# An encoder layer on one core: the output projections with eight pairs of k tiles by seven products instead of five, and weight sums formed by accumulating transfers

## The chip, the cores and the metric

The kernel runs on one core of a Trainium2 chip. The metric is the device time of one execution in microseconds (us); three runs of the kernel before gave a median of 909.48 us (908.48 to 910.48).

TensorE (PE) does the matmuls, VectorE (DVE) and ScalarE (ACT) the elementwise work, GpSimd (POOL) a few small operations, and SyncE (SP) issues the DMA transfers. Each engine works through its own queue in order; semaphores hold an instruction until what it reads, or the buffer that it writes, is ready.

## The reference

One encoder layer on 512 rows of width 1024 in float32: a feed-forward block (FFN), a mixer (a convolution and an mLSTM), and a second FFN. The change touches only the two FFNs, and in them only the second matrix product, `@ w_out`:

```python
def swiglu(x, w_in, w_out):
    gate, up = jnp.split(x @ w_in, 2, axis=-1)      # x: 512 x 1024, w_in: 1024 x 5632
    return (jax.nn.silu(gate) * up) @ w_out         # 512 x 2816 by 2816 x 1024

h = swiglu(rmsnorm(x, norm_ffn1_pre[l]), w_ffn1_in[l], w_ffn1_out[l])
x = x + FFN_RESIDUAL_SCALE * rmsnorm(h, norm_ffn1_post[l])
...
h = swiglu(rmsnorm(x, norm_ffn2_pre[l]), w_ffn2_in[l], w_ffn2_out[l])
x = x + FFN_RESIDUAL_SCALE * rmsnorm(h, norm_ffn2_post[l])
```

## The kernel before, in words

**Three matmuls for a float32 product.** Every operand is split into a high part (a cast on ScalarE, L295) and the rest (a subtraction, mostly on VectorE, L297); the product is high by high, high by low and low by high, all into one accumulator. So every weight tile and every left side passes ScalarE and VectorE once before PE may use it.

**Fewer products.** A product of two by two blocks takes seven block products instead of eight in the manner of Strassen, if sums of blocks are formed first. The first projection does that throughout (`mm_part`, L434; sums of its weights L159). The second projection, the subject here, has 22 k tiles of 128 rows. A pair of k tiles (2n, 2n+1) with the two halves of the rows and the two halves of the 1024 columns makes such a two by two product: 7 x 2 x 3 = 42 matmuls of 512 columns (`product_out`, L567), where the two plain k tiles (`mm_out`, L592) take 24 each. `SEVEN` = 5 pairs are done so, k tiles 10 to 21 plainly.

**The order.** All accumulators of the second projection fit in the eight banks of PSUM only if the products share them, so the pairs are gone through twice. In phase "a" PE does products 1, 5, 6 and 7 of all five pairs (24 matmuls each), then `taken` copies those four sums out (ScalarE copies L577 and L579, VectorE sums L534), and in phase "b" it does products 2, 3 and 4 (18 matmuls each), each pair followed by one plain k tile (10 to 14). Then come k tiles 15 and 16, and last the five k tiles 17 to 21 (`TAIL`), one block of 128 rows after the other, each followed by its norm. The list `OUT` holds this order:

```python
    OUT = [("a", i) for i in range(SEVEN)]
    for i in range(SEVEN):
        OUT += [("b", i), ("k", 2 * SEVEN + i)]
    OUT += [("k", k) for k in range(3 * SEVEN, NF)]
```

**The weights' way.** `w_load` issues the loads in the order of the list `stream` (SP, L146 and L148) into four buffers `raw` (512 KB each); `w_get` makes the high and low parts of weights loaded earlier and starts the next loads, one or two entries ahead. For a pair, call the blocks of its weight B11, B12 (first k tile, left and right columns), B21 and B22 (second). In "a" a pair loads its first k tile and the right half of the second; `w_out_a` forms B12-B11, B22-B12 and B22-(B12-B11) with three VectorE subtractions (L192), and keeps the last in a small buffer. In "b" the second k tile is loaded whole, and `w_out_b` forms B21 minus the kept one (L215).

**The left sides.** `left_a` and `left_b` form sums of column halves of the activations, 128x256 at a time (L534), and split them, for one pair at a time.

**What sets the order within an engine.** The program is written once, and a scheduler with a cost model puts each engine's instructions in an order before the kernel is built; on the chip the queues run in that order. A buffer of a pool is handed on when its last reader is done, and a load into it waits for that.

**Where it stands.** In the profiled execution PE begins the first FFN's output projection at 231.46 us; the preparation of its first weights on ScalarE and VectorE overlaps the end of the first projection.

Of the kernel before, what the change touches and what calls it, by code (L numbers as in the profile page):

```python
# [28 lines left out]
TAIL = 5  # L29
SEVEN = 5  # L30
# [8 lines left out]
def encoder_kernel(ctx: ExitStack, tc: tile.TileContext, a: dict, out: bass.AP):  # L39
# [93 lines left out]
    stream = [v if isinstance(v[0], list) else one(v) for v in stream]  # L133
    loaded, ready = [], []
    pos, done = [0], [0]

# [48 lines left out]
    kept = []  # L185

    def w_out_a(r0, r1):
# [3 lines left out]
        def sub(o, a_, b_):  # L191
            nc.vector.tensor_tensor(out=o, in0=a_, in1=b_, op=ALU.subtract)  # L192
# [12 lines left out]
        split(bh[:, c[0]], bl[:, c[0]], r1[:, c[0]])  # L205
        split(bh[:, c[1]], bl[:, c[1]], t)
        return {1: (ah[:, c[0]], al[:, c[0]]), 7: (ah[:, c[1]], al[:, c[1]]),
                5: (bh[:, c[0]], bl[:, c[0]]), 6: (bh[:, c[1]], bl[:, c[1]])}

    def w_out_b(r1):  # L210
# [4 lines left out]
        nc.vector.tensor_tensor(out=r1[:, c[0]], in0=r1[:, c[0]], in1=kept.pop(0), op=ALU.subtract)  # L215
        split(t[:, c[0]], t[:, c[1]], r1[:, c[0]])
# [221 lines left out]
    def ffn(xq, between, finish, mid=None, within=None, ahead=(2, 2, 1, 1), late=None, prep=None):  # L438
# [3 lines left out]
        h = [bigt() for _ in range((NF + 3) // 4)]  # L442

# [80 lines left out]
        ea, eb = bigt(), bigt()  # L524
# [15 lines left out]
        def parts(hi, lo, at):  # L540
            return {n: (hi[:, c:c + 256], lo[:, c:c + 256]) for n, c in at.items()}

        def left_a(i):
            a_, b_ = hcol(2 * i), hcol(2 * i + 1)
            hi, lo = halves()
            s1 = t4()[:, 0:256]
            tt(s1, a_[:, early], b_[:, early], ALU.add)
            split(hi[:, 0:256], lo[:, 0:256], a_[:, later])
            tt(a_[:, early], a_[:, later], a_[:, early], ALU.subtract)
            tt(a_[:, later], s1, a_[:, later], ALU.subtract)  # L550
            split(hi[:, 256:512], lo[:, 256:512], s1)
            split(hi[:, 512:1024], lo[:, 512:1024], a_)
            return parts(hi, lo, {1: 0, 5: 256, 7: 512, 6: 768})

        def left_b(i):
            a_, b_ = hcol(2 * i), hcol(2 * i + 1)
            hi, lo = halves()
            split(hi[:, 0:512], lo[:, 0:512], b_)
            tt(a_[:, early], b_[:, later], a_[:, later], ALU.subtract)
            split(hi[:, 512:768], lo[:, 512:768], a_[:, early])  # L560
            return parts(hi, lo, {4: 0, 2: 256, 3: 512})
# [614 lines left out]
```

## Time and profile before

| | |
|---|---|
| median of 3 runs | 909.48 us (908.48 to 910.48) |
| the profiled execution | 911.16 us |
| its span in the trace | 909.4 us |
| granted TensorE clock, whole span | 0.999 |
| bytes moved by DMA | 96.47 MB, mean 106 GB/s |
| share of the 16 DMA engines' time, loads and stores | 35.5% |

The profile gives, for each engine, the time in which it was busy; the program's work on PE is so dense that its pieces overlap, so a mean duration of one matmul (0.39 us) is longer than the distance from one to the next. Windows give the busy time of each engine in a stretch of the span, with the number of its instructions in brackets; the chain of waits is followed back from the last instruction to whatever released each step; a row of an instruction names start, duration, engine, line, operation, and output <- input, and in square brackets the idle time just before it with what ended it. `ps` are PSUM accumulators, `whi` and `wlo` high and low parts of weights, `raw` loaded weights, `big` large buffers (four times 512 columns), `t` small ones.

### The profile page before, as it was taken

The page shows a single profiled execution, that of the slowest core. Times are in us where ns is not written, and L with a number is a line of the kernel's source. Part 1 is how long each engine was busy: PE and PEld are TensorE (multiplying, and loading weights), DVE is VectorE, ACT ScalarE, POOL GpSimd, SP SyncE. Part 2 cuts the span into 40 slices and gives each one's busy share as a digit, 9 for nine tenths or more (in the row PEclk, how much of TensorE's full clock was granted, in tenths as well). Part 3 has the DMA queues.
Part 4 walks back from the last instruction along what each step waited for, and adds up shares of the span by engine and source line. Part 5 has one row for each costly group of instructions (what it writes and reads, how often), then busy time and mean ns, then how long its engine had stood idle before and what let it go on. Part 6 is the DMA issues. An engine that isn't in the chain of part 4 may idle for free.

```text
span 909.4 us, 14920 instructions
## 1 busy us (share of the span) xinstructions
PE 896.4 (99%) x5971; PEld 814.5 (90%) x5971; DVE 691.1 (76%) x1115; ACT 460.2 (51%) x807; POOL 42.5 (5%) x68
## 2 busy tenths in 40 slices
PE   9999999999999999999999999999999999999997
PEld 7999999999877888988888888999999999977885
DVE  5988988888999457474666647889888988999435
ACT  6645555555565434464555435545545545566311
POOL 5000000000001001100011000000000000000000
PEclk9999999999999999999999999999999999999999
DMA  8233434333344650433222602224443432343402
GB/s 240 85 95 116 138 96 133 100 94 105 116 140 121 188 157 1 120 91 95 71 67 73 205 0 80 61 70 117 116 117 93 121 107 88 118 146 108 161 2 92
DMA packets 126256, 96.47 MB, mean 106 GB/s; under 512 B 4181, under 2 KB 114793, under 8 KB 126186
## 3 DMA queue, kind: packets, MB, share of 16 engines
q1 hardware_dynamic: 126186, 95.51, 35.5%
q8 instruction: 47, 0.77, 0.3%
q14 instruction: 23, 0.19, 0.1%
HBM read 93.40 MB, written 2.10 MB: 105 GB/s over the span
## 4 chain that ended last, share of the span: by engine, by line
PE 91%; DVE 4%; DMA 2%; ACT 1%; issue 1%; DVEq 0%; POOLq 0%; POOL 0%; ACTq 0%
PE ps L434 39%; PE ps L592 13%; PE ps L425 12%; PE ps L567 9%; PE ps L456 5%; PE ps L1133 5%; PE ps L755 3%; DMA raw<-in_w_ffn_in_dram 2%; DVE big L297 1%; DVE wlo L297 1%; PE ps L346 1%; PE ps L1048 1%; DVE big L534 1%; ACT big L295 1%; PE ps L288 1%
## 5 line engine op out<-in xcount | busy, mean ns | idle before, releaser
L297 DVE TENSOR_TENSOR wlo<-raw,whi 128x1024 fp32r<-128x1024 f32 x203 | 240.0, 1192 | 49.3 <-ACT whi L295 25.7
L295 ACT CAST whi<-raw 128x1024 fp32r<-128x1024 f32 x207 | 207.4, 1029 | 123.6 <-DVE raw L159 48.1
L434 PE MATMUL ps<-big,whi 128*128 128x256 f32 x1920 | 264.8, 280 | 0.3 <-ACT whi L295 0.2
L434 PEld LDWEIGHTS ps<-big,whi 128*128 128x128 f32 x1920 | 243.0, 188 | 1.2 <-ACT whi L295 0.7
L434 PE MATMUL ps<-big,wlo 128*128 128x256 f32 x960 | 151.2, 280 | 0.0
L434 PEld LDWEIGHTS ps<-big,wlo 128*128 128x128 f32 x960 | 129.5, 188 | 0.0
L592 PE MATMUL ps<-whi,big 128*128 128x512 f32 x384 | 121.8, 394 | 0.4 <-ACT whi L295 0.4
L592 PEld LDWEIGHTS ps<-whi,big 128*128 128x128 f32 x384 | 71.9, 188 | 17.3 <-ACT whi L295 1.3
L425 PE MATMUL ps<-big,whi 128*128 128x512 f32 x320 | 78.3, 397 | 0.0
L567 PE MATMUL ps<-whi,big 128*128 128x512 f32 x240 | 75.2, 392 | 2.7 <-ACT big L295 2.7
L592 PE MATMUL ps<-wlo,big 128*128 128x512 f32 x192 | 75.0, 393 | 0.0
L425 PEld LDWEIGHTS ps<-big,whi 128*128 128x128 f32 x320 | 59.5, 188 | 13.7 <-issue 0.2
L434 PE MATMUL ps<-big,ws 128*128 128x256 f32 x480 | 65.3, 280 | 0.0
L434 PEld LDWEIGHTS ps<-big,ws 128*128 128x128 f32 x480 | 60.2, 188 | 0.0
L567 PEld LDWEIGHTS ps<-whi,big 128*128 128x128 f32 x240 | 44.7, 188 | 12.9 <-ACT big L295 3.5
L504 ACT COPY t<-ps 128x256 f32<-128x256 f32 x40 | 14.9, 372 | 70.9 <-PE ps L434 70.7
L295 ACT CAST big<-big 128x512 fp32r<-128x512 f32 (+2 forms) x68 | 36.1, 582 | 23.5 <-DVE big L534 10.8
L567 PE MATMUL ps<-wlo,big 128*128 128x512 f32 x120 | 44.6, 391 | 0.0
L592 PEld LDWEIGHTS ps<-wlo,big 128*128 128x128 f32 x192 | 36.1, 188 | 8.3
L297 DVE TENSOR_TENSOR big<-big,big 128x512 fp32r<-128x512 f32 (+2 forms) x68 | 40.6, 634 | 0.0
L425 PE MATMUL ps<-big,wlo 128*128 128x512 f32 x160 | 40.4, 395 | 0.0
L425 PEld LDWEIGHTS ps<-big,wlo 128*128 128x128 f32 x160 | 30.0, 188 | 7.0
(207 smaller groups left out, 1130.4 us busy)
## 6 DMA issues: line engine op xcount, KB each, us to landing
raw<-in_w_ffn_in_dram SPq DMA_DIRECT2D x88, 512.0 KB, 5.0
raw<-in_w_ffn_out_dram SPq DMA_DIRECT2D x44, 512.0 KB, 4.5
raw<-in_w_mix_in_dram SPq DMA_DIRECT2D x24, 512.0 KB, 6.0
raw<-in_w_mix_out_dram SPq DMA_DIRECT2D x8, 512.0 KB, 3.7
raw<-in_w_ffn_out_dram SPq DMA_DIRECT2D x10, 256.0 KB, 3.4
out_dram<-x SPq DMA_DIRECT2D x8, 256.0 KB, 2.0
x<-in_x_dram SPq DMA_DIRECT2D x4, 256.0 KB, 5.1
x<-in_x_dram SPq DMA_DIRECT2D x2, 512.0 KB
```

Source lines behind the costliest of these rows:

```text
L288: pin(nc.tensor.matmul(pw[:, 0:256], warm[:, 0:P], warm, start=True, stop=True))
L295: latest["hi"] = nc.scalar.copy(out=hi, in_=src)
L297: latest["lo"] = eng.tensor_tensor(out=lo, in0=src, in1=f32(hi), op=ALU.subtract)
L346: pin(nc.tensor.transpose(out=pt[:, blk(k)], in_=xs[:, blk(4 * b + k)], identity=ident))
L425: nc.tensor.matmul(o, ww[:, k, :], xk(xT, xx, k, sl), start=n == 0, stop=n == 3 * KD - 1)
L434: pin(nc.tensor.matmul(o, ww[:, k, :], x[xx][:, k, :], start=first and n == 0, stop=n == 11, skip_group_check=True))
L456: pin(nc.tensor.matmul(o, ww[:, k, :], xq_hl(xq, (k // 4, th))[xx][:, k % 4, :], start=n == 0, stop=n == 3 * KD - 1))
L504: nc.scalar.copy(a_[:, h1], x[:, h0])
L567: nc.tensor.matmul(acc[tb + t][half], left[n][x][:, blk(t)], right[n][y], start=first and x == y == 0, stop=last_ and x == 1, skip_group_c ...
L592: nc.tensor.matmul(acc[tb][half], hT[hh][:, blk(tb)], w[ww][:, blk(half, 512)], start=fresh and hh == ww == 0, stop=k == NF - 1 and hh == ...
L755: nc.tensor.matmul(pv_[i][:, 0:at.stop - at.start], xk(xT, xx, k, blk(tb)), ww[:, k % 2, at], start=n == 0, stop=n == 3 * KD - 1)
L1133: nc.tensor.matmul(acc[half], yy[yi][:, k % 4, blk(tb)], wmo[k][wi][:, blk(half, 512)], start=(n == 0 and yi == 0 and wi == 0), stop=(n == ...
```

## The change

Eight pairs (k tiles 0 to 15) are done by seven products; k tile 16 is the only plain one between, after the first pair of "b", and 17 to 21 remain the tail. The signs in the seven products are chosen anew, so that the weights' combinations are plain sums: products 1, 5, 6 and 7 use B11, B11+B12, B11+B12+B22 and B12+B22, products 2, 3 and 4 use B21, B22 and B11+B12+B21+B22.

The sums come about in transfers. SP loads B11 and B22 side by side into one `raw`, and a transfer issued by POOL with `accum_op` add then adds B12 to both (L148): the buffer holds B11+B12 and B12+B22. SP loads B11 once more by itself (L159; the first two pairs into a small `t` tile, later ones into four slots of a large one, `ring`). One VectorE addition (L225) makes B11+B12+B22 of B11 and the right half, into a kept buffer; in "b" a second accumulating transfer adds B21 to it (L164), and the second k tile is loaded whole as before. The left sides are formed for two pairs at a time, 128x2x256 in place of 128x256 (L561), into two large buffers instead of one, and `taken` subtracts where it added. The load of the gate weights for the stage that follows (`mid`) is started at the first plain k tile, now 16 instead of 12. The pools keep their sizes.

```diff
-SEVEN = 5
+SEVEN = 8
...
-        OUT += [("b", i), ("k", 2 * SEVEN + i)]
-    OUT += [("k", k) for k in range(3 * SEVEN, NF)]
+        OUT += [("b", i)] + [("k", 2 * SEVEN + i)] * (2 * SEVEN + i < NF - TAIL)
+    OUT += [("k", k) for k in range(2 * SEVEN, NF) if ("k", k) not in OUT]
...
-                stream.append(([w_out[blk(2 * n), :], w_out[blk(2 * n + 1), 512:1024]], "a"))
+                stream.append(((w_out[blk(2 * n), :], w_out[blk(2 * n + 1), :]), "a"))
...
+                if kk == "a":
+                    top, low = aps
+                    sums = rawp.tile([P, 1024], F32, tag="raw", name=nm("raw"))
+                    nc.sync.dma_start(sums[:, 0:512], top[:, 0:512])
+                    nc.sync.dma_start(sums[:, 512:1024], low[:, 512:1024])
+                    nc.gpsimd.dma_start(
+                        sums.rearrange("p (g f) -> p g f", g=2), 
+                        top[:, 512:1024].rearrange("p (g f) -> p g f", g=1).broadcast_to([P, 2, 512]), accum_op=ALU.add)
...
+                    nc.sync.dma_start(own, top[:, 0:512])
+                    raws = [own, sums]
+                    loaded.append((raws, kk))
+                    continue
+                if kk == "b":
+                    nc.gpsimd.dma_start(kept[0], aps[0][:, 0:512], accum_op=ALU.add)
...
+                    own = [kept.pop(0)]
...
-        sub(r1[:, c[0]], r0[:, c[1]], r0[:, c[0]])
-        sub(r0[:, c[1]], r1[:, c[1]], r0[:, c[1]])
-        t = t2()
-        sub(t, r1[:, c[1]], r1[:, c[0]])
+        t = keep()
+        nc.vector.tensor_tensor(out=t, in0=r0, in1=r1[:, c[1]], op=ALU.add)
         kept.append(t)
         ah, al = wt("whi"), wt("wlo")
-        split(ah, al, r0)
+        split(ah[:, c[0]], al[:, c[0]], r0)
         bh, bl = wt("whi"), wt("wlo")
-        split(bh[:, c[0]], bl[:, c[0]], r1[:, c[0]])
-        split(bh[:, c[1]], bl[:, c[1]], t)
...
+        split(bh, bl, r1)
+        split(ah[:, c[1]], al[:, c[1]], t)
...
         split(hi, lo, r1)
-        nc.vector.tensor_tensor(out=r1[:, c[0]], in0=r1[:, c[0]], in1=kept.pop(0), op=ALU.subtract)
-        split(t[:, c[0]], t[:, c[1]], r1[:, c[0]])
+        split(t[:, c[0]], t[:, c[1]], t4_)
...
         def left_a(i):
-            a_, b_ = hcol(2 * i), hcol(2 * i + 1)
-            hi, lo = halves()
-            s1 = t4()[:, 0:256]
-            tt(s1, a_[:, early], b_[:, early], ALU.add)
-            split(hi[:, 0:256], lo[:, 0:256], a_[:, later])
...
+            g, a_, b_ = group(i)
+            hi, lo = halves(g)
+            s1 = t4()[:, 0:256 * g].rearrange("p (g f) -> p g f", g=g)
+            tt(s1, a_[:, :, early], b_[:, :, early], ALU.subtract)
+            split(hi[:, :, 0:256], lo[:, :, 0:256], a_[:, :, later])
...
-                if n == 12 and mid:
+                if plain_n == 1 and mid:
                     mid()
```

**VectorE at the end of the first projection of the first FFN.** The first pairs' weight sums stand among the splits of the last first-projection weights (`wlo_27..` and `ws_..`) and the rows that finish its results (L506 to L512, later L531 to L537). A name in the last brackets is a semaphore waited for: DMAHW one of SP's transfers, DMASW one of POOL's. Before:

```order
L192 TENSOR_TENSOR raw_2871<-raw_2869 128x512 [waits DMAHW3_49]
L297 TENSOR_TENSOR ws_372_2759<-t_369_2750,ws_372_2759 128x512 [waits Activation_49]
L511 TENSOR_TENSOR t_365_2651<-ps_2647,t_365_2651 128x256 [waits PE_49]
L159 TENSOR_TENSOR raw_2746<-t_369_2750,raw_2746 128x512 [waits DVE_49]
L192 TENSOR_TENSOR raw_2869<-raw_2871,raw_2869 128x512 [waits DMAHW4_49,DVE_49]
L512 TENSOR_TENSOR big_230<-t_365_2651,t_366_2652 128x256 [waits DVE_49]
L159 TENSOR_TENSOR raw_2746<-raw_2746 128x512 [waits DVE_49]
L508 TENSOR_TENSOR t_382_2775<-ps_2772,t_380_2773 128x256 [waits PE_49]
L297 TENSOR_TENSOR wlo_2763<-raw_2746,whi_2762 128x1024 [waits Activation_49]
L487 TENSOR_TENSOR big_230<-ps_2647,t_366_2652 128x256 [waits PE_49]
```

and now:

```order
L186 TENSOR_TENSOR raw_2746<-raw_2746 128x512 [waits DVE_49]
L225 TENSOR_TENSOR big_231<-t_384_2873,raw_2869 128x512 [waits DMAHW6_49,DMASW0_49]
L533 TENSOR_TENSOR t_382_2775<-ps_2772,t_380_2773 128x256 [waits PE_49]
L225 TENSOR_TENSOR big_231<-t_384_2873,raw_2886 128x512 [waits DMAHW0_49,DMASW1_49]
L321 TENSOR_TENSOR wlo_2763<-raw_2746,whi_2762 128x1024 [waits Activation_49]
L512 TENSOR_TENSOR big_230<-ps_2647,t_366_2652 128x256 [waits PE_49]
L321 TENSOR_TENSOR wlo_2767<-raw_2748,whi_2766 128x1024 [waits Activation_49]
L321 TENSOR_TENSOR wlo_2877<-t_384_2873,whi_2876 128x512 [waits PE_49,Activation_49]
L531 TENSOR_TENSOR t_382_2775<-ps_2771,t_380_2773 128x256 [waits PE_49]
L321 TENSOR_TENSOR wlo_2877<-big_231,whi_2876 128x512 [waits Activation_49]
L536 TENSOR_TENSOR t_381_2774<-ps_2770,t_381_2774 128x256 [waits PE_49]
```

The two additions for pairs 0 and 1 (L225) wait for a transfer of POOL each, and stand ahead of the low parts of the first projection's last weights and of the rows that finish its results.

**POOL's queue** had nothing of the output projection. Now, between its last work in the first projection and the gate weights' cast, it begins with:

```order
L321 TENSOR_TENSOR wlo_305<-raw_103,whi_304 128x1024 [waits DMAHW2_49,Activation_49]
L148 DMA raw_2869<-in_w_ffn_out_dram 128x2x512 [waits DMAHW3_49,DMAHW5_49,DMAHW1_49,DMAHW6_49,DVE_49,Pool_49]
L148 DMA raw_2886<-in_w_ffn_out_dram 128x2x512 [waits DMAHW2_49,DMAHW4_49,DMAHW0_49,DMAHW7_49,DVE_49,Pool_49]
L148 DMA raw_3061<-in_w_ffn_out_dram 128x2x512 [waits DMAHW2_49,DMAHW1_49,DMAHW3_49,DVE_49,Pool_49]
L164 DMA big_231<-in_w_ffn_out_dram 128x512 [waits DVE_49]
L148 DMA raw_3113<-in_w_ffn_out_dram 128x2x512 [waits DMAHW4_49,DMAHW3_49,Pool_49]
L164 DMA big_231<-in_w_ffn_out_dram 128x512 [waits DVE_49]
L148 DMA raw_3153<-in_w_ffn_out_dram 128x2x512 [waits DMAHW5_49,DMAHW0_49,DMASW0_49]
L148 DMA raw_3206<-in_w_ffn_out_dram 128x2x512 [waits DMAHW3_49,DMAHW4_49,DMASW1_49,DVE_49]
L164 DMA big_3023<-in_w_ffn_out_dram 128x512 [waits DVE_49,PE_49]
```

The accumulating transfers of both phases share this one queue, those for "b" (L164) between those for "a" (L148), each waiting for the loads that it adds to or for the split that read the kept sum.

**VectorE at the switch from "a" to "b" in the first FFN.** The rows that take the finished products out read `ps` (L534, later L561). Before:

```order
L297 TENSOR_TENSOR wlo_3235<-raw_3232,whi_3234 128x1024 [waits DMAHW5_49,PE_49,Activation_49]
L534 TENSOR_TENSOR big_228<-big_228 128x256 [waits DVE_49]
L215 TENSOR_TENSOR raw_3232<-raw_3232,t_385_2875 128x512 [waits DVE_49]
L534 TENSOR_TENSOR big_3025<-ps_3021,big_3025 128x512 [waits PE_49,Activation_49]
L534 TENSOR_TENSOR big_3025<-ps_3022,big_3025 128x512 [waits PE_49,Activation_49]
L297 TENSOR_TENSOR wt_3236<-raw_3232,wt_3236 128x512 [waits Activation_49]
L534 TENSOR_TENSOR big_3026<-ps_3023,big_3025 128x512 [waits DVE_49,PE_49]
L534 TENSOR_TENSOR big_3026<-ps_3024,big_3025 128x512 [waits DVE_49,PE_49]
L297 TENSOR_TENSOR wlo_3285<-raw_3282,whi_3284 128x1024 [waits DMAHW6_49,Activation_49]
L297 TENSOR_TENSOR big_3276<-big_226,big_3276 128x512 [waits Activation_49]
```

and now:

```order
L321 TENSOR_TENSOR wlo_3345<-raw_3342,whi_3344 128x1024 [waits DMAHW3_49,PE_49,Activation_49]
L321 TENSOR_TENSOR wt_3346<-big_231,wt_3346 128x512 [waits DMASW3_49,Activation_49]
L321 TENSOR_TENSOR wlo_3395<-raw_3392,whi_3394 128x1024 [waits DMAHW4_49,PE_49,Activation_49]
L321 TENSOR_TENSOR wlo_3402<-raw_3399,whi_3401 128x1024 [waits DMAHW5_49,PE_49,Activation_49]
L321 TENSOR_TENSOR wt_3403<-big_231,wt_3403 128x512 [waits DMASW5_49,Activation_49]
L321 TENSOR_TENSOR big_3386<-big_226,big_3385 128x2x512 [waits Activation_49]
L321 TENSOR_TENSOR big_3386<-big_226,big_3385 128x2x256 [waits Activation_49]
L561 TENSOR_TENSOR big_3022<-ps_3018,big_3022 128x512 [waits PE_49]
L561 TENSOR_TENSOR big_3022<-ps_3019,big_3022 128x512 [waits PE_49,Activation_49]
L321 TENSOR_TENSOR big_3426<-big_230,big_3426 128x512 [waits Activation_49]
L561 TENSOR_TENSOR big_3023<-ps_3020,big_3022 128x512 [waits DVE_49,PE_49]
```

Before, one weight split of "b" (`wlo_3235`) stood ahead of the first row that reads a finished product; now the splits of the first two pairs of "b" and of k tile 16, and the first left side of "b", stand there.

More of the change, by code (lines that the diff above doesn't have):

```diff
@@ L132, in encoder_kernel @@
                 stream.append(rows(w_out, n * P))
-    stream = [v if isinstance(v[0], list) else one(v) for v in stream]
-    loaded, ready = [], []
+    stream = [v if isinstance(v[0], (list, tuple)) else one(v) for v in stream]
+    loaded, ready, ring, own2 = [], [], [], []
     pos, done = [0], [0]
@@ L142, in w_load @@
                 raws = []
+                if kk == "a":
[6 more added lines that the diff above has]
+                        top[:, 512:1024].rearrange("p (g f) -> p g f", g=1).broadcast_to([P, 2, 512]), accum_op=ALU.add)
+                    if ring:
+                        own = ring.pop(0)
+                        ring.append(own)
+                    else:
+                        if not own2:
+                            v = t4()
+                            own2.extend(v[:, blk(i, 512)] for i in range(2))
+                        own = own2.pop(0)
+                    nc.sync.dma_start(own, top[:, 0:512])
[4 more added lines that the diff above has]
+                    nc.gpsimd.dma_start(kept[0], aps[0][:, 0:512], accum_op=ALU.add)
+                    aps = [aps[0]]
+                    own = [kept.pop(0)]
+                else:
+                    own = []
                 for ap in aps:
@@ L442, in ffn @@
         h = [bigt() for _ in range((NF + 3) // 4)]
+        spare.extend(h[-1][:, q, 0:512] for q in (2, 3))
         def act(j, pg, pu):
@@ L523, in ffn @@
         later, early = slice(256, 512), slice(0, 256)
-        ea, eb = bigt(), bigt()
+        ea, eb, xb = bigt(), bigt(), bigt()
+        ring[:] = [xb[:, q, 0:512] for q in range(4)]
+        spare.extend(eb[:, q, 0:512] for q in (2, 3))
         extra = {
@@ L555, in left_b, with halves @@
-        def left_b(i):
[L556 to L561, printed above, removed]
+        def halves(g):
+            if g == 1:
+                t = bigt(F32R).rearrange("p q f -> p (q f)")
+                return t[:, 0:1024].rearrange("p (g f) -> p g f", g=1), t[:, 1024:2048].rearrange("p (g f) -> p g f", g=1)
+            return tuple(
+                bigt(F32R).rearrange("p q f -> p (q f)")[:, 0:2048].rearrange("p (g f) -> p g f", g=2) for _ in range(2))
@@ new lines, in parts, with group @@
+        def parts(hi, lo, g, at):
+            return [{n: (hi[:, i, c:c + 256], lo[:, i, c:c + 256]) for n, c in at.items()} for i in range(g)]
+        def group(i):
+            g = min(2, SEVEN - i)
+            v = h[i // 2].rearrange("p (g e) f -> p g e f", e=2)[:, 0:g, :, 0:512]
+            return g, v[:, :, 0], v[:, :, 1]
+        def left_a(i):
+            g, a_, b_ = group(i)
[3 more added lines that the diff above has]
+            split(hi[:, :, 0:256], lo[:, :, 0:256], a_[:, :, later])
+            tt(a_[:, :, early], a_[:, :, later], a_[:, :, early], ALU.subtract)
+            tt(a_[:, :, later], a_[:, :, early], b_[:, :, early], ALU.add)
+            split(hi[:, :, 256:512], lo[:, :, 256:512], s1)
+            split(hi[:, :, 512:1024], lo[:, :, 512:1024], a_)
+            return parts(hi, lo, g, {1: 0, 5: 256, 7: 512, 6: 768})
@@ L563, in product_out @@
+        def left_b(i):
+            g, a_, b_ = group(i)
+            hi, lo = halves(g)
+            split(hi[:, :, 0:512], lo[:, :, 0:512], b_)
+            tt(a_[:, :, early], b_[:, :, later], a_[:, :, later], ALU.subtract)
+            split(hi[:, :, 512:768], lo[:, :, 512:768], a_[:, :, early])
+            return parts(hi, lo, g, {4: 0, 2: 256, 3: 512})
         def product_out(n, left, right, first, last_):
@@ L619, in ffn @@
             else:
-                left, right = left_b(n), w_get(2)
+                if n % 2 == 0:
+                    lefts = left_b(n)
+                left, right = lefts[n % 2], w_get(2)
                 for m in (2, 3, 4):
                     product_out(m, left, right, n == 0 and m == 4, False)
+        ring.clear()
         def whole(tb):
```

33 lines of the change are left out of this document (13 added, 20 removed).

## The prediction

> **What bounds the kernel now.** I read the page first, then windows of the output projection, then the chain of waits, then single rows of VectorE (DVE).
>
> ```profile
> span 909.4 us, 14920 instructions
> PE 896.4 (99%) x5971; PEld 814.5 (90%) x5971; DVE 691.1 (76%) x1115; ACT 460.2 (51%) x807; POOL 42.5 (5%) x68
> ```
>
> TensorE (PE) is busy 99% of the span, so a removed matmul is worth its share of PE's time as long as PE is fed. The change touches only the two output projections (231 to 346 us in the first FFN, 548.3 us later in the second).
>
> ```profile
> 246.36 1.41 PE ps L434 x12
> 247.77 16.83 PE ps L567 x74
> ...
> 287.25 4.10 PE ps L567 x18
> 291.36 5.53 PE ps L592 x24
> ...
> 306.58 4.10 PE ps L567 x18
> ```
>
> These pieces of the chain give PE's price where it never waits: a matmul of the sevens (L567) 4.10/18 = 0.228 us, a plain one (L592) 5.53/24 = 0.230, one of the first projection (L434) 1.41/12 = 0.118. They overlap, so the 0.39 us of a single row is not the price. From the first L567 to the end of the chain's L567 piece at 310.68 PE has 5 x 42 matmuls of the sevens, 4 x 24 plain ones and 48 of L434: 47.8 + 22.1 + 5.6 = 75.6 us of work.
>
> ```profile
> 231.46 0.40 PE L567 MATMUL ps<-whi,big 128*128 128x512 f32 x1
> ...
> core 0: us, PE busy (x), PEclk, DMA share, GB/s
> 231.40:310.70 79.30, 76.77 (x357) 1.00 0.44 137
> 779.70:859.00 79.30, 76.77 (x356) 1.00 0.43 142
> ```
>
> The stretch takes 310.68 - 231.46 = 79.2 us, so **PE loses 3.6 us there in each FFN** (busy time shows 2.5 of it, since a waiting PE's last matmul is still counted). The clock is 1.00 throughout. Where it is lost:
>
> ```profile
> 255.00:261.00 6.00, 6.00 (x28) 4.97 (x27) 6.00 (x11) 4.03 (x6) 0.00 (x0) 1.00 0.57 195
> 261.00:267.00 6.00, 4.67 (x21) 3.54 (x20) 3.80 (x7) 4.81 (x10) 0.00 (x0) 1.00 0.27 79
> 273.00:279.00 6.00, 5.54 (x25) 4.18 (x23) 6.00 (x12) 3.17 (x7) 0.00 (x0) 1.00 0.00 0
> 279.00:285.00 6.00, 5.27 (x22) 3.98 (x23) 6.00 (x9) 4.54 (x7) 0.00 (x0) 1.00 0.37 111
> ```
>
> (PE, PEld, DVE, ACT, POOL, clock, DMA share, GB/s.) A full window holds 28 matmuls; three hold 21, 25 and 22: 16 missing x 0.228 = 3.6 us, all at the switch from the first half of the sevens ("a") to the second ("b"). DVE is full there: it is the late engine.
>
> **What changes, part by part.**
>
> *PE.* Three more pairs take 3 x 42 = 126 matmuls x 0.228 = 28.7 us; six fewer plain k tiles give back 6 x 24 = 144 x 0.230 = 33.2. That is **-4.5 us per FFN, -9.0 in all** (996 matmuls become 960). The minimum gain if nothing else moves.
>
> *DVE.* Its price is the distance between starts:
>
> ```profile
> 247.48 0.68 DVE L192 TENSOR_TENSOR raw<-raw,raw 128x512 f32<-128x512 f32 x1
> 248.09 0.69 DVE L192 TENSOR_TENSOR t<-raw 128x512 f32<-128x512 f32 x1
> 248.69 0.42 DVE L534 TENSOR_TENSOR big<-t,big 128x256 f32<-128x256 f32 x1
> ...
> 259.66 1.21 DVE L297 TENSOR_TENSOR wlo<-raw,whi 128x1024 fp32r<-128x1024 f32 x1
> 260.80 0.41 DVE L534 TENSOR_TENSOR big<-big 128x256 f32<-128x256 f32 x1
> 261.13 0.68 DVE L215 TENSOR_TENSOR raw<-raw,t 128x512 f32<-128x512 f32 x1
> ```
>
> So 0.60 us for 512 columns, 1.14 for 1024, 0.33 for 256. An "a" pair before: three weight differences 1.8, lows 1.14 + 0.60 + 0.60, left side five of 0.33 and one of 0.60: 6.4 us, against 24 x 0.228 = 5.5 us on PE. DVE loses the race in "a", and everything it owes for "b" comes after the switch. After: one sum 0.60, the same lows 2.34, and a left side shared by two pairs (five of 0.60, one of 1.14, halved: 2.07): **5.0 us against 5.5**. DVE wins by 0.5 us a pair, eight times. In "b" a pair goes from 3.6 to 2.9 us, against 4.1 on PE. The order shows the effect: the splits of the first two "b" pairs, of k16 and their left side now stand ahead of the first read of the finished "a" products. So the 3.6 us can go; whether they all do depends on what now stands in DVE's way. The paired left side holds two `big` tiles, the sums one more, at places that PE has let go by then; the tail of five k tiles is unchanged, and its weights are wanted over 4.8 us (21 matmuls) after its start.
>
> *SP.* The first two pairs' B11 halves are loaded early, in the tile that the sums of x have left:
>
> ```profile
> 32.77 1.22 DVE L364 TENSOR_TENSOR big<-big,t 128x1024 f32<-128x1024 f32 x1
> ...
> 35.16 0.37 SPq L148 DMA_DIRECT2D raw<-in_w_ffn_in_dram  x1
> ```
>
> That reader ends at 34.0, two issues take 0.7 us, and the next load of SP was due at 35.16 anyway: nothing. Later ring loads stand behind the wait for pair 0's buffer, which the load of pair 4 would wait for as well: nothing. The gate weights' 64 KB load moves from k12 to k16, with 22 us of PE's work left before it is read: nothing.
>
> *The accumulating transfers.* No transfer before is issued by POOL, and none adds, so the time T from a landed load to a landed sum is unknown. Nearest rows:
>
> ```profile
> raw<-in_w_ffn_out_dram SPq DMA_DIRECT2D x44, 512.0 KB, 4.5
> raw<-in_w_ffn_out_dram SPq DMA_DIRECT2D x10, 256.0 KB, 3.4
> ```
>
> Below, T is a 512 KB load, 4.5 us; above, twice that, 9.0, for a transfer that reads the old bytes as well. I take 6, nearer the row. What T costs is set by the DVE queue, in order, where each sum's add stands ahead of work that PE waits for.
>
> ```profile
> 213.93 1.48 SPq L146 DMA_DIRECT2D raw<-in_w_ffn_out_dram  x2
> ...
> 218.04 0.69 DVE L192 TENSOR_TENSOR raw<-raw 128x512 f32<-128x512 f32 x1 [0.33 <-DMA raw<-in_w_ffn_out_dram]
> ...
> 230.04 1.10 PE L434 MATMUL ps<-big,whi 128*128 128x256 f32 x8
> ```
>
> The second pair's buffer is free at 213.93 + 1.48 - 0.33 = 215.1; its two 256 KB loads land at 215.1 + 0.3 + 3.4 = 218.8, its sum at 218.8 + T. Its add (0.60) is followed by 4.5 us of DVE rows up to L536, the result PE wants at 230.04. So the add must start by 225.0: **T up to 6.2 us costs nothing at the front**, beyond it us for us. DVE already waited for the load there (0.33 us). ScalarE's casts of these sums wait too, but before its next evacuation it has until 225. The second tight place is the add for pair 6: its buffer (pair 2's) comes free near 246, so its sum is there at 249.7 + T, and 4.1 us of DVE rows behind that add make pair 4's last weights, which PE reaches near 262: free up to T = 8.2. POOL's queue also holds the accumulations for "b"; they wait for a split of the same pair and come before the next pair's, and DVE has done those splits 6 us or more ahead.
>
> T = 6 therefore costs nothing; T = 9 costs 2.8 + 0.8 = 3.6 us per FFN. The Trainium skill, "DMA: Bandwidth & Descriptors", section "Anatomy of one DMA — SWDGE (gpsimd) path", puts a POOL-issued transfer at about 2.0 us plus bytes/436e3 per us; an estimate by that page is 3.2 us for 512 KB, which would leave the same sum. The case shows no such transfer.
>
> **The sum.** 2 x 4.5 for the matmuls, and 2 x 3.6 at the switch less what stays or comes new. Bounds for that rest: nothing, and all of the 3.6. I take half, 1.8: the scheduler's order for before lost 3.6 at one handover, and this order has two new ones (front, pair 6) whose room is 0.2 to 2 us. So 9.0 + 2 x 1.8 = **12.6 us**. The profiled execution took 911.16 us (span 909.4), 1.7 more than the median 909.48; it becomes 898.6, and the median **896.9, say 897.0**.
>
> **Rivals.**
> - *The old wait stays* (the copies and sums of the finished products gate "b" whatever DVE has done before): only the matmuls count, 900.5. For it: PE's idle 1.33 us at the switch ended with ScalarE. Against: the chain from 264.6 to 280.5 is DVE work that now stands earlier.
> - *All of the wait goes*: 909.5 - 16.2 = 893.3.
> - *The sums land late, and it is slower.* One mechanism: T. Beyond 8.2 both places cost, (T - 6.2) + (T - 8.2) per FFN; it eats 4.5 + 3.6 = 8.1 us at T = 11.3. At T = 14, 13.6 per FFN: 920.5. For it, the DMA engines' load:
>
> ```profile
> 297.00:303.00 6.00, 6.00 (x28) 4.91 (x27) 3.59 (x3) 3.19 (x4) 0.00 (x0) 1.00 0.82 261
> ...
> 321.00:327.00 6.00, 6.00 (x28) 4.89 (x27) 3.58 (x3) 2.01 (x3) 0.00 (x0) 1.00 1.08 329
> ```
>
>   By these a full set moves some 310 GB/s. An "a" pair now needs 768 KB of loads and 768 KB of sums in 5.5 us: 288 GB/s if a sum costs like a load, 430 if it costs double. The first is just carried; the second falls back 2.1 us a pair, 12.7 over the six pairs that are not loaded ahead, less the 17 us between the first load and the third pair's turn on PE. At three times the price it is 28 less 17: 11 us per FFN, slower. So it takes a price near three.
> - *DVE keeps POOL from preparing transfers.* DVE is full here (6.00 of 6.00 above). If POOL could prepare only while DVE stands, each of eight sums would hold DVE for T = 6: 48 us on top of 8 x 5.0 against 43.7 on PE, 44 us per FFN, about 980. The Trainium skill, "SBUF — State Buffer", section "Who interferes with whom", says that a VectorE instruction in a two-port mode locks POOL out and starves such transfers, but that a two-input one, as all here are, meets only POOL's reads; by that rule this does not happen. No run here shows it yet.
> - *It doesn't do what it says*: the counts (960 matmuls, 16 sums in place of 40 differences) stand in the built order, so only the time can fail. At T near 11 it is even.
>
> **How the numbers follow.** Forecast (893.5 to 900): 0.52. All of the wait gone and a little more: 0.06. Old wait stays, or T of 9 to 10 (900 to 907.7): 0.18. Even: 0.06. Late sums: 0.14; POOL locked out: 0.04. A measurement of this kernel tells about 0.2% (1.8 us) from no change. Faster by more: 0.76; within: 0.06; slower: 0.18. The range leaves out the slow cases and a little below: 892.5 to 909.0.
>
> **What would show it.** 960 matmuls of L602 and L627; PE at 0.228 us through "a" with windows of 28; no short windows at the switch. DVE's waits at L225 (the adds) for a DMA: under 1 us beyond the front if T is near 6, several us each if late. The DMA list's time to landing for L148: 5 to 7. Wrong if those rows show 11 or more, if PE's short windows move into "a" behind DVE's L225, or if windows at the switch still hold 21 to 25.

## The result

The changed kernel took **930.58 us** (median of 4 runs, 929.2 to 931.93) against 909.88 us before in the same comparison: a ratio of 1.023 (95% interval 1.0209 to 1.025), slower by 2.3%. Forecast were 897.0 us and a range up to 909.0.

The page of the changed kernel, its span and busy times:

```profile
span 928.2 us, 14985 instructions
PE 898.7 (97%) x5935; PEld 815.3 (88%) x5935; DVE 695.2 (75%) x1079; ACT 471.0 (51%) x803; POOL 80.8 (9%) x100
```

The 36 matmuls are gone (5935 instead of 5971), yet PE is busy 2.3 us longer. Span less busy time is PE's idle time: 29.5 us, 13.0 before. The mean clock fell from 0.999 to 0.985. So of the 18.8 us by which the span grew, 16.5 are idle, and the forecast 9.0 us of saved matmuls were more than eaten by 11.3 us that the others took longer at a lower clock. Where, in windows of the first FFN (PE, PEld, DVE, ACT, POOL, clock, DMA share, GB/s):

```profile
231.00:237.00 6.00, 0.00 (x0) 0.00 (x0) 5.17 (x8) 0.89 (x3) 0.00 (x0) 0.77 0.34 111
237.00:243.00 6.00, 5.99 (x35) 5.99 (x36) 5.94 (x11) 4.37 (x9) 2.15 (x2) 0.66 0.75 158
...
261.00:267.00 6.00, 4.63 (x10) 3.00 (x10) 3.34 (x5) 4.08 (x6) 1.36 (x2) 0.54 0.84 144
267.00:273.00 6.00, 5.71 (x16) 4.53 (x17) 4.65 (x7) 1.51 (x3) 2.16 (x2) 0.60 0.66 166
273.00:279.00 6.00, 6.00 (x28) 4.99 (x27) 4.06 (x6) 3.71 (x7) 0.86 (x1) 1.00 0.79 177
279.00:285.00 6.00, 6.00 (x28) 4.95 (x28) 6.00 (x10) 2.63 (x3) 2.13 (x2) 1.00 0.86 172
```

The loss sits at the front and in phase "a". From 273 us on the windows hold 28 matmuls again. (The second FFN loses about as much: PE's idle time grows by 8.2 us between 213 and 345 us and by some 7.4 from 775 us on.) At the switch, which now lies near 300 us and cost 3.6 us before, 0.17 us of a gap are left. What PE waited for shows the chain of single rows, PE first (start, duration, idle time before and what ended it):

```profile
237.01 2.08 PE L458 MATMUL ps<-big,whi 128*128 128x256 f32 x8 [6.21 <-DVE t L536]
256.26 1.21 PE L458 MATMUL ps<-big,whi 128*128 128x256 f32 x8 [0.59 <-DVE t L536]
262.14 0.79 PE L602 MATMUL ps<-wlo,big 128*128 128x512 f32 x1 [3.27 <-DVE wlo L321]
```

VectorE's rows, then POOL's:

```profile
225.94 0.69 DVE L225 TENSOR_TENSOR big<-t,raw 128x512 f32<-128x512 f32 x1 [5.16 <-DMA raw<-in_w_ffn_out_dram]
226.56 0.42 DVE L533 TENSOR_TENSOR t<-ps,t 128x256 f32<-128x256 f32 x1
231.79 0.69 DVE L225 TENSOR_TENSOR big<-t,raw 128x512 f32<-128x512 f32 x1 [4.82 <-DMA raw<-in_w_ffn_out_dram]
```

```profile
220.01 1.37 POOL L148 DMA_DIRECT2D raw<-in_w_ffn_out_dram  x1 [196.49 <-DVE raw L186]
226.18 1.24 POOL L148 DMA_DIRECT2D raw<-in_w_ffn_out_dram  x1 [4.80 <-issue]
237.81 1.21 POOL L148 DMA_DIRECT2D raw<-in_w_ffn_out_dram  x1 [10.39 <-DMA raw<-in_w_ffn_out_dram]
238.54 1.42 POOL L164 DMA_DIRECT2D big<-in_w_ffn_out_dram  x1
```

Pair 0's sum is issued at 220.01 and has landed at 225.94. Pair 1's transfer is not issued until 226.18, right after that, though "issue" says that POOL waited for nothing the profile shows; its sum is there at 231.79. VectorE has stood for both, and PE, which wanted the result behind it (L536) at 230.8, stands 6.21 us. Over the whole execution VectorE's additions waited:

```profile
  DMA raw<-in_w_ffn_out_dram: 44.5, 15
```

That is 44.5 us in 15 waits at L225. A small transfer starts 0.73 us after a large one (238.54 after 237.81), a second large one never beside a first: the first suspicion is a limit on what may be under way.

### The profile page after: what moved, and what is told of

Same layout as the page of the kernel before. It is cut to its first block, busy times and chain, and to the rows that moved or that the text cites. A ratio compares the mean times of both kernels' runs of the same rounds, so it can differ in the third digit from the quotient of the medians.

```text
span 928.2 us, 14985 instructions
## 1 busy us (share of the span) xinstructions
PE 898.7 (97%) x5935; PEld 815.3 (88%) x5935; DVE 695.2 (75%) x1079; ACT 471.0 (51%) x803; POOL 80.8 (9%) x100
## 3 DMA queue, kind: packets, MB, share of 16 engines
q1 hardware_dynamic: 129354, 97.09, 35.3%
q0 software_dynamic: 6656, 12.58, 8.1%
## 5 line engine op out<-in xcount | busy, mean ns | idle before, releaser
L319 ACT CAST whi<-raw 128x1024 fp32r<-128x1024 f32 x197 | 202.1, 1051 | 121.4 <-DVE raw L186 47.7
L321 DVE TENSOR_TENSOR wlo<-raw,whi 128x1024 fp32r<-128x1024 f32 x193 | 234.0, 1221 | 34.8 <-ACT whi L319 18.3
L458 PEld LDWEIGHTS ps<-big,wlo 128*128 128x128 f32 x960 | 131.1, 190 | 0.0
L602 PE MATMUL ps<-whi,big 128*128 128x512 f32 x384 | 125.2, 403 | 1.7 <-ACT big L319 1.5
L602 PEld LDWEIGHTS ps<-whi,big 128*128 128x128 f32 x384 | 74.1, 194 | 19.7 <-ACT big L319 2.7
L602 PE MATMUL ps<-wlo,big 128*128 128x512 f32 x192 | 76.5, 407 | 8.5 <-DVE wlo L321 8.5
L627 PE MATMUL ps<-whi,big 128*128 128x512 f32 x192 | 60.9, 393 | 0.0
L148 POOL DMA_DIRECT2D raw<-in_w_ffn_out_dram x16 | 19.7, 1231 | 472.6 <-DVE wlo L321 207.1
L319 ACT CAST big<-big 128x512 fp32r<-128x512 f32 (+1 forms) x48 | 37.0, 801 | 17.5 <-DVE big L561 14.2
L627 PEld LDWEIGHTS ps<-whi,big 128*128 128x128 f32 x192 | 36.0, 188 | 8.0
L321 DVE TENSOR_TENSOR big<-big,big 128x512 fp32r<-128x512 f32 (+1 forms) x48 | 42.6, 913 | 0.2 <-PE ps L602 0.2
L534 ACT ACTIVATE t<-t 128x512 f32<-128x512 f32 x40 | 25.2, 631 | 31.1 <-DVE t L531 29.0
```

The source lines that it names most:

```text
L148: nc.gpsimd.dma_start(sums.rearrange("p (g f) -> p g f", g=2), top[:, 512:1024].rearrange("p (g f) -> p g f", g=1).broadcast_to([P, 2, 512 ...
L319: latest["hi"] = nc.scalar.copy(out=hi, in_=src)
L321: latest["lo"] = eng.tensor_tensor(out=lo, in0=src, in1=f32(hi), op=ALU.subtract)
L458: pin(nc.tensor.matmul(o, ww[:, k, :], x[xx][:, k, :], start=first and n == 0, stop=n == 11, skip_group_check=True))
L534: nc.scalar.activation(c, c, AF.Silu)
L602: nc.tensor.matmul(acc[tb + t][half], left[n][x][:, blk(t)], right[n][y], start=first and x == y == 0, stop=last_ and x == 1, skip_group_c ...
```

## The experiments

All times are medians, beside the kernel before in the same comparison (909.9 to 910.9 us).

**Space for descriptors.** The program reserves 1024 bytes per partition in which POOL prepares its transfers. Three runs gave more.

```diff
-    nc = _bacc.Bacc("TRN2", ..., dynamic_dma_scratch_size=1024)
+    nc = _bacc.Bacc("TRN2", ..., dynamic_dma_scratch_size=1408)
```

> The changed kernel with one number changed: the space kept for the descriptors of POOL's transfers, 1408 in place of 1024 bytes per partition. Every engine's instructions stand in the same order. In the changed kernel's trace the second sum (L148 at 226.18) starts only when the first has landed (225.9), though its loads were there some 5 us earlier, and a small one (L164 at 238.54) starts 0.73 us after a large one (237.81). Theory A, the space is full with one 512 KB sum: with 1.4 times the space two fit, the second L148 starts within 2 us of the first (by 222 us) and lands by 229, the first gap of PE (6.21 us in each FFN) falls under 3 us, and the time to 905 to 922. Theory B, each accumulating transfer waits for the one before for another reason (its semaphore, the DMA engines' queue): nothing moves, 929 to 932.

913.87 us, ratio 1.0036 (1.0024 to 1.0048). POOL's rows:

```profile
216.79 1.38 POOL L148 DMA_DIRECT2D raw<-in_w_ffn_out_dram  x1 [195.20 <-DVE t L536]
218.33 1.21 POOL L148 DMA_DIRECT2D raw<-in_w_ffn_out_dram  x1 [0.16 <-issue]
```

The second sum follows 1.54 us after the first, and PE's first gap falls from 6.21 to 2.36 us. Theory A holds: with the order of all instructions unchanged, this one number takes 16.7 us off. It does not bring back the forecast.

```diff
-    small = ctx.enter_context(tc.tile_pool(name="small", bufs=4))
+    small = ctx.enter_context(tc.tile_pool(name="small", bufs=3))
...
-    nc = _bacc.Bacc("TRN2", ..., dynamic_dma_scratch_size=1024)
+    nc = _bacc.Bacc("TRN2", ..., dynamic_dma_scratch_size=1600)
```

> The changed kernel with 1600 bytes for descriptors, the instructions of every engine in the same order (one small pool has three buffers instead of four). With 1024 bytes one 512 KB sum fitted beside a 256 KB one, with 1408 two did. If the space still costs at 1408 (913.87 us; one L148 stood 5.91 us): 902 to 910. If by now a sum's own time (6 to 7 us from issue to landing) and the DMA engines' load decide: 911 to 916.

914.53 us (1.0046, 1.0029 to 1.0063): 1600 bytes gain nothing over 1408. A run with 3072 bytes was paid for with a small buffer, which moved instructions:

```diff
-    t2p = ctx.enter_context(tc.tile_pool(name="t2p", bufs=6))
+    t2p = ctx.enter_context(tc.tile_pool(name="t2p", bufs=5))
...
-    nc = _bacc.Bacc("TRN2", ..., dynamic_dma_scratch_size=1024)
+    nc = _bacc.Bacc("TRN2", ..., dynamic_dma_scratch_size=3072)
```

> The changed kernel with 3072 bytes for POOL's descriptors (1024 in the changed kernel, 1408 in the run before, which took 913.87 us), paid for with one small buffer of 2 KB less (five t2 instead of six), which also moves some instructions. In the run with 1408 one L148 still stood 5.91 us behind earlier ones (start 244.37), and the DMA engines' share was 1.03 to 1.09 from 237 to 255 us. If the space still bounds it: that wait goes, the PE gap of 2.67 us at 251 goes, 900 to 908. If the DMA engines bound it by now: the waits stay as waits for landing, 911 to 916.

920.82 us (1.0122), above both expectations: fewer buffers cost more than the space gave, or the order did; not separated. Its trace says more than its time. POOL's idle time before its transfers that the profile gives no reason for ("issue") falls from 47.1 us in the changed kernel to 13.9 with 1408 bytes, the same with 1600, and 0.5 here. VectorE's additions (L225) still wait 39.3 us for transfers, against 45.7 in the changed kernel and 30.6 with 1408 bytes. So with room for all of them it is the landing of the sums that VectorE waits for.

**The sums taken out, or written instead of added.**

```diff
-                    nc.gpsimd.dma_start(
-                        sums.rearrange("p (g f) -> p g f", g=2), 
-                        top[:, 512:1024]. ... .broadcast_to([P, 2, 512]), accum_op=ALU.add)
...
-                    nc.gpsimd.dma_start(kept[0], aps[0][:, 0:512], accum_op=ALU.add)
```

> The changed kernel without its accumulating transfers, with nothing in their place: B12 is not added to B11 and B22, nor B21 to the kept sum, so the output projections are computed from other weights. All loads, VectorE's additions (L225), splits, left sides and matmuls stay. It shows what eight pairs give if the sums cost nothing. If the forecast's price for the rest was right (12.6 us under the kernel before), 894 to 901. If eight pairs lose by themselves, by VectorE's work, the paired left sides or the loads (six windows of PE short without any transfer), 904 or more.

894.21 us (0.9813, 0.9797 to 0.983), inside the expected 894 to 901: matmuls, VectorE's work and paired left sides were priced well.

```diff
-  ... .broadcast_to([P, 2, 512]), accum_op=ALU.add)
+  ... .broadcast_to([P, 2, 512]))
...
-                    nc.gpsimd.dma_start(kept[0], aps[0][:, 0:512], accum_op=ALU.add)
+                    nc.gpsimd.dma_start(kept[0], aps[0][:, 0:512])
```

> The changed kernel with POOL's transfers writing instead of adding (B12 replaces B11 and B22, B21 the kept sum, so the output projections are computed from other weights); same bytes, same order of every engine's instructions, 1024 bytes for descriptors. Theory, the addition is the price: a transfer that adds reads the old bytes too and takes two places per row in the descriptor space; without it two 512 KB transfers fit, the second L148 starts within 2 us of the first, a transfer lands in 3.5 to 5 us instead of 5.7, and the time is 900 to 912 (894.21 without these transfers). Rival, a transfer issued by POOL is late whatever it does: second L148 some 6 us after the first as before, 925 to 931.

898.27 us (0.9856, 0.9835 to 0.9876), a little better than the theory expected, and 32 us under the change with every instruction in the same place. The DMA queues of its page, behind those of the changed kernel (packets, MB, share of 16 engines; q0 is POOL's):

```profile
q1 hardware_dynamic: 129354, 97.09, 35.3%
q0 software_dynamic: 6656, 12.58, 8.1%
```

```profile
q0 software_dynamic: 3584, 12.58, 4.1%
```

The same 12.58 MB take 8.1% of 928.2 us = 75.2 us of all engines when they add and 4.1% of 896.7 = 36.8 us when they write: 167 and 342 GB/s, where SP's loads in the changed kernel make 97.09 MB / 327.7 us = 296. Adding costs 1.8 times a load, 2.0 times a write. Its transfers land sooner too (median from issue, of the change and of this run):

```profile
raw<-in_w_ffn_out_dram POOLq DMA_DIRECT2D x16, 512.0 KB, 5.7
```

```profile
raw<-in_w_ffn_out_dram POOLq DMA_DIRECT2D x16, 512.0 KB, 4.8
```

This run also has half the packets, so the next one adds in larger pieces:

```diff
-                        sums.rearrange("p (g f) -> p g f", g=2), 
-                        top[:, 512:1024]. ... .broadcast_to([P, 2, 512]), accum_op=ALU.add)
+                        sums,
+                        top, accum_op=ALU.add)
```

> The changed kernel with 1024 bytes for descriptors, where the large accumulating transfer adds the whole first k tile, 1024 columns of a row in one piece, instead of B12 twice (the output projections are then computed from other weights); the bytes and the first FFN's order stay, the small accumulating transfers too. The run that writes instead of adding had half the packets (3584 against 6656) beside not adding. If the number of pieces is the price: two large transfers fit the space, the second L148 starts within 2 us of the first, and the time is 898 to 912. If the reading of the old bytes is the price, whatever the pieces: the second L148 still stands for the first, 915 to 931.

918.64 us (1.0086, 1.0065 to 1.0106). The two halves of the question come apart:

```profile
220.03 1.04 POOL L148 DMA_DIRECT2D raw<-in_w_ffn_out_dram  x1 [196.47 <-DVE raw L186]
221.27 0.87 POOL L148 DMA_DIRECT2D raw<-in_w_ffn_out_dram  x1 [0.20 <-issue]
```

```profile
q0 software_dynamic: 4608, 12.58, 8.0%
```

With fewer, larger pieces two sums are under way in the old 1024 bytes, so the pieces of an addition are what fills the space; but the engines' share stays at 8.0%, so that price belongs to the addition, whatever the pieces. The time does not come down to the 913.87 us of 1408 bytes: a later L148, at 250.50, still follows 7.57 us of "issue", and PE then stands 5.78 us. And the engines are full at a lower rate. A window of the run with 1600 bytes, then one of the run that writes (columns as above):

```profile
249.00:255.00 6.00, 3.41 (x21) 2.73 (x21) 2.71 (x5) 0.00 (x0) 2.15 (x2) 1.00 1.07 184
```

```profile
237.00:243.00 6.00, 6.00 (x34) 5.16 (x33) 6.00 (x10) 3.66 (x6) 0.06 (x1) 1.00 1.01 370
```

**Fewer pairs, and the sums on VectorE.**

```diff
-SEVEN = 8
+SEVEN = 5
```

> The changed kernel with five pairs instead of eight: accumulating transfers, new signs and paired left sides stay. If the transfers are what costs, the first gap of PE stays (6 us and a low clock after it, 8 to 10 us per FFN) and the later ones become fewer: 918 to 932. If the three further pairs are what costs: 905 to 912.

929.85 us (1.0212): with five pairs the transfers cost as much.

```diff
+        add(r1[:, c[0]], r0[:, c[0]], r0[:, c[1]])
+        add(r0[:, c[1]], r0[:, c[1]], r1[:, c[1]])
         t = keep()
-        nc.vector.tensor_tensor(out=t, in0=r0, in1=r1[:, c[1]], op=ALU.add)
+        add(t, r1[:, c[0]], r1[:, c[1]])
...
         split(hi, lo, r1)
+        nc.vector.tensor_tensor(out=t4_, in0=t4_, in1=r1[:, c[0]], op=ALU.add)
```

> Eight pairs, the new signs and the paired left sides, but no accumulating transfer: the weight sums are formed by VectorE (three additions for an a pair, one for b), the weights loaded as in the kernel before. If the transfers alone made it slow, VectorE needs 3 x 0.60 + 2.34 + 2.07 = 6.2 us per a pair against 5.5 on PE, falls 0.7 x 8 = 5.6 us back at the switch (4.5 before), and the time is 909.5 - 9.0 + 2 x (0 to 1.5) = 900 to 904. If eight pairs or the paired left sides cost by themselves, 920 or more.

910.81 us (1.0002, 0.999 to 1.0013), between the two expectations. VectorE is the late engine, as said (6.00 of 6.00 us in both windows below), but its deficit does not wait for the switch; PE runs dry in the middle of "a", and its clock with it:

```profile
249.00:255.00 6.00, 5.50 (x24) 4.04 (x23) 6.00 (x10) 4.49 (x6) 0.00 (x0) 1.00 0.36 124
255.00:261.00 6.00, 4.08 (x12) 2.94 (x11) 6.00 (x9) 0.95 (x1) 0.00 (x0) 0.73 0.33 113
```

> Five pairs, sums by VectorE, no accumulating transfer: what is left of the change is the signs and the left sides formed for two pairs at a time. Per a pair VectorE saves 0.2 us (6.2 for 6.4): if pairing costs nothing, 907 to 910. If the larger pieces of the left sides come too late (a pair's first product waits for both pairs' sums), over 912.

905.35 us, ratio 0.994 (0.9925 to 0.9955), with `SEVEN = 5` beside the edit above: better than expected, and the fastest version found that computes the layer.

> Six pairs, all sums on VectorE, no accumulating transfer (five pairs took 905.35 us, eight 910.81). By the matmuls alone a further pair saves 2 x 6 x 0.23 = 2.8 us: 902.5. By VectorE's deficit of 0.7 us per further pair and FFN, paid once more at PE's lower clock after a gap, it saves nothing: 905 to 908.

906.77 us (0.9965): the sixth pair saves nothing. Five pairs again, with left sides for one pair at a time:

```diff
-                if n % 2 == 0:
-                    lefts = left_a(n)
-                left, right = lefts[n % 2], w_get(1)
+                left, right = left_a(n)[0], w_get(1)
...
```

> Five pairs, sums on VectorE, new signs, but the left sides formed for one pair at a time as in the kernel before (905.35 us with two at a time). If the pairing is what made that run faster than the kernel before, 908 to 911; if the signs and the order they bring are, 904 to 907.

907.27 us (0.9962, 0.995 to 0.9975; the paired one 0.9925 to 0.9955). So the larger part of the gain on the kernel before comes with what else is new, the signs, the places of the kept sums and the order that they bring (not separated), and about 2 us with the pairing, though the intervals overlap.

**Mixtures.** All are made of the edits above, chosen by pair (`ACC`, `BACC`: pairs whose sums in "a" and "b" come by transfer). The first two have eight pairs and 1408 bytes.

```diff
+ACC = (2, 3, 4, 5, 6, 7)
+BACC = (0, 1, 2, 3, 4, 5, 6, 7)
```

> 1408 bytes, and the sums of the first two pairs of each FFN formed by VectorE (three additions, loads as in the kernel before); pairs 2 to 7 and all of phase b by accumulating transfers. If the front is lost to the time of a transfer (PE gap 2.36 us and half clock after it, 4 to 5 us per FFN in the run with 1408 bytes), 904 to 908. If VectorE's four more additions there (2.4 us) are as late as the sums were, or the loss only moves to pairs 2 to 6, 911 or more.

908.78 us (0.9987, 0.9976 to 0.9999): the front is mended, but PE then stands 3.09 and 1.47 us near 250 us behind the sums of pairs 2 and 3. Part of the loss only moved.

```diff
+ACC = (3, 5, 7)
+BACC = (3, 4, 5, 6, 7)
```

> 1408 bytes, eight pairs; only pairs 3, 5 and 7 get their sums in a, and pairs 3 to 7 in b, by accumulating transfers, the others by VectorE. VectorE's a phase is then 5 x 6.2 + 3 x 5.0 = 46.0 us against 43.7 on PE (49.6 with all sums on VectorE, 910.81 us), and the transfers' bytes less than half. If VectorE's deficit alone is what cost 910.81, the deficit falls from 5.6 to 2.3 us and the time to 900 to 906. If single transfers among VectorE's work hold up its queue as before, 909 or more.

918.71 us (1.0099): worse than with more transfers or none. In the first FFN two of the three single sums hold up VectorE's queue, by 4.41 and 6.33 us, and PE behind it:

```profile
260.48 0.80 PE L637 MATMUL ps<-wlo,big 128*128 128x512 f32 x1 [3.79 <-DVE wlo L356]
280.41 0.79 PE L637 MATMUL ps<-wlo,big 128*128 128x512 f32 x1 [5.39 <-DVE wlo L356]
```

```diff
-SEVEN = 8
+SEVEN = 5
+ACC = ()
+BACC = (0, 1, 2, 3, 4, 5, 6, 7)
```

> Five pairs with the a sums on VectorE (as the run of 905.35 us), but the sum of b by an accumulating transfer of 256 KB, which has all of phase a to land. VectorE saves 5 x 0.60 us per FFN in b, where PE waits 0.4 to 1.9 us: 903 to 905.5 if those transfers are hidden; 907 or more if VectorE waits for them.

> As the run before with six pairs (906.77 us with all sums on VectorE). If VectorE's work at the switch is what eats the 2.8 us that a further pair saves: 902 to 905. If VectorE's deficit in phase a decides (0.7 us a pair, untouched by this): 905.5 to 908.

906.45 us (0.9953) and 907.78 us (0.9968): sums that have a whole phase to land cost at most about a microsecond, and gain nothing either.

**The sums on POOL itself.**

```diff
-        add(r1[:, c[0]], r0[:, c[0]], r0[:, c[1]])
-        add(r0[:, c[1]], r0[:, c[1]], r1[:, c[1]])
+        add(nc.gpsimd, r1[:, c[0]], r0[:, c[0]], r0[:, c[1]])
+        add(nc.gpsimd, r0[:, c[1]], r0[:, c[1]], r1[:, c[1]])
```

> Eight pairs, no accumulating transfer: POOL itself adds the first two sums of an a pair and the sum of b (in the kernel before, its four additions of 128x1024 took 2.4 us each, so 1.2 us for 128x512), VectorE adds the third. VectorE is then as light as in the change (5.0 us per a pair), a sum is there about 2.4 us after its load instead of 6 to 12. If the lateness of the sums was the whole loss: 896 to 902. If POOL's and VectorE's additions hold each other up (VectorE's rows longer than 0.69 us for 512 columns beside them), 908 or more.

> As the run with sums on POOL, with seven pairs: by the matmuls 2 x 6 x 0.23 = 2.8 us more than with eight, if nothing waits; less than with eight if the last pairs wait for VectorE.

> As the run with sums on POOL, with six pairs: 5.5 us more than with eight if nothing waits; against six pairs with all sums on VectorE (906.77 us) it is 2 to 4 us less if VectorE's deficit of 0.7 us a pair was what PE waited for at the switch, and the same if not.

927.78 (1.0185), 925.96 (1.0168) and 919.8 us (1.0099). Two neighbouring rows of VectorE in the first of them, beside an addition of POOL from 244.23 to 247.91 and without one:

```profile
247.01 1.45 DVE L543 TENSOR_TENSOR big<-big 128x512 f32<-128x512 f32 x1
...
250.09 0.68 DVE L543 TENSOR_TENSOR t<-big 128x512 f32<-128x512 f32 x1
```

The two engines hold each other up: VectorE's row doubles, and POOL's additions in "a" of the first FFN take 1.29 to 3.68 us where 1.2 were reckoned.

## Why the prediction was wrong

The steps on **PE and VectorE were right.** The run that writes instead of adding, in the same order, has a span of 896.7 us, 12.7 under the kernel before: 10.2 of PE's busy time (886.2 us) and 2.5 of idle time, where the prediction said 9.0 and 3.6. The windows at the switch hold 28 matmuls, as it said they would (the first finished product is read at 282.23 us):

```profile
PE 886.2 (99%) x5935; PEld 807.3 (90%) x5935; DVE 694.8 (77%) x1079; ACT 471.5 (53%) x803; POOL 64.5 (7%) x100
279.00:285.00 6.00, 6.00 (x28) 4.95 (x28) 6.00 (x9) 6.00 (x10) 0.00 (x0) 1.00 0.74 254
285.00:291.00 6.00, 6.00 (x28) 4.93 (x27) 6.00 (x9) 3.64 (x6) 0.00 (x0) 1.00 0.27 87
```

The step that failed is **"T = 6 therefore costs nothing"**, the time from a landed load to a landed sum. It failed in three ways. Rows of the changed kernel for the first two, SP's loads of pair 1, then VectorE's split that frees a buffer and SP's first load of pair 2:

```profile
216.51 0.38 SPq L146 DMA_DIRECT2D raw<-in_w_ffn_out_dram  x1
216.95 0.42 SPq L147 DMA_DIRECT2D raw<-in_w_ffn_out_dram  x1
...
232.40 1.22 DVE L321 TENSOR_TENSOR wlo<-raw,whi 128x1024 fp32r<-128x1024 f32 x1
233.64 0.33 SPq L146 DMA_DIRECT2D raw<-in_w_ffn_out_dram  x1
```

- *One transfer was priced, not two behind each other.* A single sum took 5.9 us from its issue (220.01 to 225.94), as taken. But pair 1's sum could not be prepared until pair 0's had landed. Its loads, issued at 216.5 and 216.95, would be there near 221 (an estimate: SP's loads in the run with 1408 bytes land within 4.1 us of their issue, since POOL's transfer follows), so its T was about 10.8, beyond the upper bound of 9.0. The prediction had the first place right to the microsecond: an addition that should start 5.0 us before PE wants L536, here by 225.8, started at 231.79, 6.0 late, and PE's gap was 6.21. More space mends this: 16.7 us.
- *The price of an adding transfer.* The rival of late sums reckoned with once, twice and three times a load, and set against it 17 us of lead. The price was 1.8 (in time of the DMA engines), but the lead was not there: loads start only when a buffer is free, and pair 2's, due well before, was issued at 233.64, since its buffer waited for a split on VectorE that stood behind the late addition (L321 at 232.40). So lateness fed itself. Writing in place of adding takes 15.6 us off the run with 1408 bytes. How much of that is DMA engine time and how much the later landing (4.8 us against 5.7, 6.7 with more under way) was not separated.
- *PE's clock was left out of every price.* Windows of 2 to 5 us around the first two gaps (PE, clock, DMA share, GB/s):

```profile
230.00:234.00 4.00, 0.80 (x7) 1.00 0.32 57
234.00:237.00 3.00, 0.00 (x0) 0.54 0.64 215
237.00:241.00 4.00, 3.99 (x18) 0.50 0.63 139
241.00:243.00 2.00, 2.00 (x19) 0.99 0.99 196
...
262.00:266.00 4.00, 3.86 (x9) 0.50 0.98 153
266.00:271.00 5.00, 4.48 (x11) 0.50 0.68 196
271.00:273.00 2.00, 2.00 (x9) 0.81 0.82 136
```

In both gaps the clock falls to half, and PE's next matmuls run at half speed: for 4 us after the first gap, for 9 us after the second, in which a short wait recurs. With 5.4 and 3.4 us after the gaps of 3.58 and 3.11 us in the second FFN that makes 21.9 us of work at half clock, so some 11 us lost: nearly all of the 11.3 us by which PE's busy time is above 887.4 (896.4 less 9.0). The Trainium skill, "TensorE: Matmul & The Clock Gate", section "What's actually happening", describes this: half clock after an idle window of about 3.4 us, full clock after a busy one of that length; the first gap agrees (half clock from some 3.4 us after 230.80, where PE stopped, and full clock 4.0 us after 237.01), and the second shows that coming back can take more than twice as long. Other runs differ from the first figure, and there the measurement decides: after gaps of 2.36 and 2.67 us (1408 bytes) and 1.93 us (sums on VectorE) PE ran some 3 us at half clock too, while after 2.47 us (whole rows) and 3.09 us (first two pairs on VectorE) the clock stayed at 1.00. So the length of a gap alone does not tell. In the output projections before, no gap was longer than 1.33 us, and the clock stayed at 1.00.

Of the rivals, **late sums** was the one that came, with a chance of 0.14; by its own numbers T near 11 is even with the kernel before. What it had not counted: against the run that writes, in the same order, PE is idle 19.0 us longer (29.5 and 10.5) and busy 12.5 us longer (898.7 and 886.2), so most of the loss is waits, those behind the first late sum included, and the clock made it larger. Of the signs that the prediction named, the time from issue to landing looked right (5.7 us, in 5 to 7) although the sums were late, because a late issue does not show in it; the waits at L225 and the short windows in "a" did show it. **Locked out by VectorE** did not come: POOL's issue took 1.2 to 1.4 us whether VectorE was full (5.94 of 6.00 in 237 to 243) or stood. The rule quoted from the Trainium skill, "SBUF — State Buffer", section "Who interferes with whom", agrees there, and its other half, that two-input VectorE work meets POOL's reads, agrees with the runs that add on POOL.

The prediction's estimate by the Trainium skill, "DMA: Bandwidth & Descriptors", section "Anatomy of one DMA — SWDGE (gpsimd) path", 3.2 us for 512 KB, was below the medians measured here, 4.8 us for a write and 5.7 for an addition.

## What to carry to other kernels

A transfer that adds is not a load with a sum for free: here it cost twice a write in DMA engine time, and its small pieces filled the space for descriptors, so that sums queued one behind another. Price it by its arrival behind the one before it, in the queue of the engine that must wait, and move it only where it has a phase of slack; there it was hidden here to within about a microsecond, and gained nothing. Where TensorE has been busy throughout, a gap can cost a second time: four gaps of 3.1 to 6.2 us were followed here by 3.4 to 9.1 us of work at half clock, so a range should be wider on that side.

## What the runs showed of the hardware that was not expected

An addition fills the space for POOL's descriptors by its pieces: 1024 bytes held one addition of 256 rows of 2 KB and a smaller one, but two when the rows were 4 KB (second issue 1.24 us after the first instead of 6.17). The run that writes, with the old pieces but half the packets, also had two under way (issues at 219.36 and 220.88). A sum wanted at once by an engine with an in-order queue can make few transfers worse than many: three pairs by transfer took 918.71 us, six took 908.78.
